# A two-layer recurrent decoder trunk: delayed stores, later residual loads, a third weight buffer and whole-tile output-weight loads

## The chip, the cores and the metric

The kernel runs on one core of one Trainium2 chip. The metric is device time in microseconds of one execution; the runs of the kernel before took 1116.57 us in the median of three (1116.24 to 1118.81). A separate execution was profiled and took 1120.96 us, of which 1119.2 us lie between its first and its last instruction.

## The reference

Two layers are applied to a prompt of 512 tokens and to 8 samples of one token each, with the same weights. Every recurrence is causal and also returns its new state.

```python
def even_layer(h, ...):                       # layer 0
    u = rmsnorm(h, pre_g)
    proj = u @ w_in                           # q,k,v and gates of 8 delta-rule heads, 4 GLA heads
    qkv = silu(causal_conv(...)); q, k = l2norm(q), l2norm(k)
    o1, s_gdn = gated_delta_chunked(q, k, v, beta, log_g, S0)
    o2, s_gla = gla_chunked(q, k, v, log_a, S0)
    o = concat(rmsnorm(o1) * silu(g1), rmsnorm(o2) * silu(g2)) @ w_out
    return h + rmsnorm(o, post_g)

def odd_layer(h, ...):                        # layer 1
    z, xbc, dt = split(rmsnorm(h, pre_g) @ w_in)
    x, B, C = silu(causal_conv(xbc))
    y, s_ssd = ssd_chunked(x, dt, A, B, C, h0)    # 32 heads of 64, 4 groups, state 128
    y = grouped_rmsnorm((y + d * x) * silu(z))
    return h + rmsnorm(y @ w_out, post_g)
```

## The kernel before, in words

**Projections.** All matrix products of the trunk go through `project_half`: a weight tile of 1024 x 128 (eight 128 x 128 blocks) is multiplied with one half of the tokens, 256 or 264 columns, by three products for each block (high part of the weight times high and low part of the activation, low part of the weight times high part: lines 267, 268, 269). That is 24 matmuls for a half and 48 for a tile. A tile comes from memory as one 512 KB load into a `raw` buffer (`load_w`, line 173), of which there are two; `split_w` makes its high part on ScalarE (line 251) and its low part on VectorE or GpSimd (helper `tt`, line 145), into `w` buffers, of which there are five. Output-weight tiles are loaded by `load_wk` (line 228) as two pieces of 256 KB.

**The order of the work.** The program is written per head and per group, but the order in which each engine executes is made when the program is built: a scheduler of the framework sorts every engine's instructions by its own estimate of when they are ready. Each engine then executes its list strictly in that order. All transfers of the kernel are issued by SyncE (SP), so SP's list is one queue: a transfer that has to wait for data or for a free buffer holds up all that stand behind it, weight loads among them. `tc.issue_after(x)` tells the scheduler to place an instruction behind x on x's engine.

**States of the samples.** Each head or pair of heads of the eight samples has a state of 512 KB that is loaded into an `st` buffer, updated and stored from it again. There are two `st` buffers. In layer 0 they hold, in turn, the matrices of `gdn_blocks` (lines 625 to 637, a block inversion that GpSimd does in some 60 small steps), the GLA states (load line 944, use by TensorE line 946, store line 953), and the delta-rule states (load line 770, use line 774, store line 801). In layer 1 `ssd_group` handles four pairs of heads for each of four groups: `sample_state` loads a state (line 1281), multiplies it on GpSimd into `sb` (line 145), scales it on ScalarE (line 1290), adds on VectorE and stores it (line 1292). States of groups 0 to 2 are handled inside the group, those of the last group at the start of the output projection.

**Layer 1, prompt.** In `ssd_group` the inputs of a pair are projected and convolved (`conv`, VectorE line 148), transposed on TensorE (line 1321), scaled by the step (to `ch`, line 1328 or 145), multiplied by the decay on GpSimd (to `ap`), and used in matmuls at lines 1348 and 1361. The normalized outputs of groups 0 to 2 go to a scratch array `ydr` (line 1415), to be read back in the output projection.

**Output projection.** `out_project` contracts 2048 channels in two halves of 1024 (`ks[0]`, `ks[1]`). Layer 0's halves are channels 0 to 3 with 8 to 11 and 4 to 7 with 12 to 15, in units of 128; layer 1's are 0 to 7 and 8 to 15. `mid()` stands between: for layer 0 it handles the last four delta-rule states, then `conv_states` (lines 463 to 470: transposes of the convolution tail through the single PSUM buffer `ps`, a copy to one of two `row` buffers, and stores) and `conv_history` (lines 417 to 420: three small state loads into `st`, each transposed through the same `ps` buffer). `add()` asks for the residual rows that are added at the very end.

Of the kernel before, what the change touches and what calls it, by code (L numbers as in the profile page):

```python
# [16 lines left out]
P = 128  # L17
D = 1024
NK = D // P
TP = 512  # L20
# [37 lines left out]
def kernel(  # L58
# [46 lines left out]
    dma = nc.sync.dma_start  # L105
# [4 lines left out]
    psm = ctx.enter_context(tc.tile_pool(name="psm", bufs=1, space=bass.MemoryType.PSUM))  # L110

    BUFS = {
        "raw": 2, "w": 5, "ua": 16, "ub": 16, "kq": 8, "ap": 8, "vg": 8, "f1": 4, "pre": 3, "inv": 4, "ch": 5, "of": 4, "dec": 5, "hp": 1, "tail": 1, "kqg": 2, "sg": 2,
        "st": 2, "sb": 2, "smc": 6, "smp": 4, "sms": 9, "jk": 1, "c5": 4, "c2": 1, "jd": 1, "nss": 1, "nrs": 1, "ors": 3, "smt": 1, "s1": 3, "u1": 2, "s2": 3, "smh": 6, "sp": 2, "row": 2,
    }
    npo = [0]
    phase = [0]
# [40 lines left out]
    def load_rows(main, extra, tags, between=None):  # L158
# [9 lines left out]
                rows[i].append(xt)  # L168
        return rows

    def load_w(w, row0, col0):
        raw = sb([P, NK, P], tag="raw")
        dma(raw, w[row0:row0 + D, col0:col0 + P].rearrange("(k p) c -> p k c", p=P))
        return raw

    def xblock(rows, i, k):
# [46 lines left out]

    def load_wk(w, ks, col0):
        raw = sb([P, NK, P], tag="raw")
        for h in range(2):
            src = w[ks[4 * h] * P:(ks[4 * h] + 4) * P, col0:col0 + P]
            dma(raw[:, 4 * h:4 * h + 4], src.rearrange("(k p) c -> p k c", p=P))
        return raw

    nsplit = [2]
# [339 lines left out]
    kq, am, eg = {}, {}, {}  # L571
# [468 lines left out]
    def out_project(w, dr, smp, ks, gname, rtags, ptags, mid, add, ltags, share, last, done):  # L1040
# [9 lines left out]
                part.append([t.bitcast(F32) for t in split_tile(ptags[i])])  # L1050
            act.activation(part[i][b], project_half(wts[i], rhs, b), AF.Copy)
        rhs = load_rhs(dr, smp, ks[1], rtags[1], "dec", 2)
        rows = add()
        acc = sb([P, T], tag="ch")
        rs = sb([P, NC + 1], tag="ors")
        low, obs, wts, sqs, ogs, sums = {}, {}, {}, {}, {}, {}
# [9 lines left out]
        for i, b in [(i, b) for i in range(NK - late) for b in range(2)] + [(i, b) for b in range(2) for i in range(NK - late, NK)]:  # L1066
            if b == 0:
                wts[i] = split_w(load_wk(w, ks[1], i * P), *lates.get(i, ()))
            if b == 0 or i >= NK - late:
                sqs[i] = sb([P, T], tag="f1") if i else acc  # L1070
                ogs[i] = sb([P, T], tag="ch")
# [153 lines left out]
    def ssd_group(g):  # L1225
# [52 lines left out]
        def sample_state(j):  # L1278
            pr = 4 * g + j
            st = sb([P, NS, P], tag="st")  # L1280
            dma(st, state_ssd[0, :, 2 * pr:2 * pr + 2].rearrange("b h p n -> (h p) b n"))
            tmp = sb([P, NS, P], tag="sb")
            for q in range(2):
                tt(pool, tmp[:, 4 * q:4 * q + 4], bcb[1][q], st[:, 4 * q:4 * q + 4], MULT)
            dve.reduce_sum(ysr[:, j], tmp, axis=mybir.AxisListType.X)
            tmp = sb([P, NS, P], tag="sb")
            for q in range(2):
                tt(pool, tmp[:, 4 * q:4 * q + 4], bcb[0][q], bc3(xds[:, j, 4 * q:4 * q + 4], P), MULT)
            for b in range(NS):
                act.activation(st[:, b], st[:, b], AF.Copy, scale=sc2[:, 1, pr, b:b + 1])  # L1290
            tt(dve, st, st, tmp, ADD)
            dma(ssd_s[0, :, 2 * pr:2 * pr + 2].rearrange("b h p n -> (h p) b n"), st)
            if j == 3:
                gs = slice(4 * g, 4 * g + 4)
                ya = sb([P, 4, NS], tag="sms")
                tt(pool, ya, ysr, sc2[:, 1, gs], MULT)
                tt(pool, ysm[:, gs], ysm[:, gs], ya, ADD)
                if g % 2 == 1:
                    sample_norm(g)
# [80 lines left out]
        for j in range(4):  # L1380
            pr = 4 * g + j
            y = yt[j][:, 0:TP]
            gt = gts[j]
            el = sb([P, TP], tag="pre")
            for hh in range(2):
                dma(el[hh * 64:hh * 64 + 64, :], ldr[2 * pr + hh:2 * pr + hh + 1, :].to_broadcast([64, TP]))
            act.activation(el, el, AF.Exp)
# [23 lines left out]
        for j in range(4):  # L1411
            y = yt[j][:, 0:TP]
            stt(y, y, vec("ssdg", 4 * g + j, True), rs, MULT, MULT)
            if g < SG - 1:
                dma(ydr[4 * g + j], y)
            else:
                kept[4 * g + j] = yt[j]

# [53 lines left out]
```

## Time and profile before

| | us |
|---|---|
| median of 3 runs | 1116.57 |
| profiled execution | 1120.96 |
| its span, first to last instruction | 1119.2 |
| TensorE matmul busy | 1048.8 |
| TensorE weight load busy | 1006.4 |
| VectorE busy | 720.3 |
| ScalarE busy | 627.4 |
| GpSimd busy | 535.7 |

The mean granted TensorE clock is 0.972. TensorE is busy in 94% of the span, and each of the other engines in 48 to 64%. So a row of another engine matters only where TensorE waited for it. The stages are, in time: layer 0 up to its output projection (to about 490 us), that projection and the norm (to about 700 us), the groups of layer 1 (to about 1046 us), and the last output projection.

A waiting row in the timeline ends in brackets: how long the engine was idle before it, and who released it. In the table of waits the numbers are the total in us, how many times, and the longest.

### The profile page before, as it was taken

Reading aid. Unit: us, or ns where it says so; the run is one execution under the profiler, and the core shown is the slowest. Engines: PE = TensorE matmul, PEld = TensorE weight load, DVE = VectorE, ACT = ScalarE, POOL = GpSimd, SP = SyncE. Lnnn points to the kernel's source line nnn. Section 1 sums busy time; section 2 is a strip of 40 time slices with the busy share of each in tenths; the row PEclk is TensorE's granted clock in tenths of the full one; section 3 lists DMA queues with packets and bytes.
Section 4 is the critical chain, followed back from the end, with each engine's and each line's share of the span. In section 5 each row is a group of like instructions: output and inputs, shape, how many; then the busy total and the mean of one; then the engine's idle time right before and its main releaser. Section 6 shows DMA issues by size and latency. Waiting matters only on the chain.

```text
span 1119.2 us, 23031 instructions
## 1 busy us (share of the span) xinstructions
PE 1048.8 (94%) x8900; PEld 1006.4 (90%) x8900; DVE 720.3 (64%) x1207; ACT 627.4 (56%) x1518; POOL 535.7 (48%) x701
## 2 busy tenths in 40 slices
PE   8999979999989989999889999998999999999997
PEld 7999979899989989889888988898998988989997
DVE  5798353655867754565645366698787688778543
ACT  5566445544444645546233465775686676775452
POOL 4034961304124377114435362386469477468632
PEclk8999999999999989989998999999999999999999
DMA  5234245622554424745563351755657556657632
GB/s 166 81 92 110 72 139 153 194 59 78 171 145 124 110 70 130 217 137 146 160 197 115 100 170 39 210 146 144 188 170 198 181 161 194 206 177 216 187 90 78
DMA packets 241732, 160.01 MB, mean 143 GB/s; under 512 B 21463, under 2 KB 221358, under 8 KB 241606
## 3 DMA queue, kind: packets, MB, share of 16 engines
q1 hardware_dynamic: 241622, 158.53, 48.9%
q8 instruction: 70, 1.15, 0.4%
q14 instruction: 40, 0.33, 0.1%
HBM read 127.05 MB, written 31.84 MB: 142 GB/s over the span
## 4 chain that ended last, share of the span: by engine, by line
PE 40%; DMA 17%; POOL 15%; DVE 13%; ACT 8%; issue 4%; SPq 2%; DVEq 0%; POOLq 0%; ACTq 0%
PE pj L267 9%; PE pj L268 9%; PE pj L269 9%; POOL sb L145 6%; POOL st L145 3%; ACT dec L1343 2%; DVE w L145 2%; DMA sb<-ud 2%; DMA st<-in_state_ssd_dram 2%; DMA out_dram<-st 2%; DVE f L148 1%; DMA pre<-ldr 1%; POOL w L145 1%; DMA inv<-bd 1%; PE px L268 1%
## 5 line engine op out<-in xcount | busy, mean ns | idle before, releaser
L267 PE MATMUL pj<-ua,w 128*128 128x256 f32 x776 | 228.3, 295 | 4.5 <-ACT ua L342 1.7
L269 PE MATMUL pj<-ua,w 128*128 128x256 f32 x776 | 226.9, 293 | 1.2 <-DVE w L145 1.2
L267 PE MATMUL pj<-ub,w 128*128 128x264 f32 x768 | 226.5, 295 | 1.4 <-ACT ub L342 0.9
L269 PE MATMUL pj<-ub,w 128*128 128x264 f32 x768 | 225.7, 294 | 0.0
L268 PE MATMUL pj<-ub,w 128*128 128x264 f32 x742 | 219.0, 295 | 0.0
L268 PE MATMUL pj<-ua,w 128*128 128x256 f32 x750 | 217.7, 291 | 0.0
L145 DVE TENSOR_TENSOR w<-raw,w 128x1024 fp32r<-128x1024 f32 x102 | 136.2, 1335 | 62.9 <-PE pj L268 33.9
L267 PEld LDWEIGHTS pj<-ua,w 128*128 128x128 f32 x776 | 151.3, 195 | 7.4 <-ACT ua L342 2.0
L251 ACT ACTIVATE w<-raw 128x1024 fp32r<-128x1024 f32 x123 | 130.0, 1057 | 46.9 <-DMA raw<-in_o_w_out_dram 11.1
L269 PEld LDWEIGHTS pj<-ua,w 128*128 128x128 f32 x776 | 151.5, 195 | 3.1 <-DVE w L145 1.4
L267 PEld LDWEIGHTS pj<-ub,w 128*128 128x128 f32 x768 | 148.2, 193 | 2.6 <-ACT ub L342 1.1
L269 PEld LDWEIGHTS pj<-ub,w 128*128 128x128 f32 x768 | 148.1, 193 | 1.8 <-issue 1.5
L268 PEld LDWEIGHTS pj<-ua,w 128*128 128x128 f32 x750 | 146.7, 196 | 0.2
L268 PEld LDWEIGHTS pj<-ub,w 128*128 128x128 f32 x742 | 143.3, 193 | 1.6 <-issue 1.1
L145 POOL TENSOR_TENSOR w<-raw,w 128x1024 fp32r<-128x1024 f32 x20 | 49.7, 2484 | 49.1 <-PE px L268 19.4
L145 POOL TENSOR_TENSOR sb<-inv,st 128x512 f32<-128x512 f32 x32 | 54.3, 1714 | 22.7 <-DMA inv<-bd 13.7
L148 DVE SCALAR_TENSOR_TENSOR pf<-xr,cvw,pf 128x512 f32<-128x512 f32 x72 | 54.0, 750 | 11.6 <-ACT pf L440 10.7
L148 DVE SCALAR_TENSOR_TENSOR f<-xr,cvw,f 128x512 f32<-128x512 f32 x72 | 57.6, 799 | 4.3 <-ACT f L440 3.6
L145 POOL TENSOR_TENSOR sms<-sms,sms 128x16 f32<-128x16 f32 (+2 forms) x56 | 22.1, 396 | 77.0 <-ACT sms L960 41.9
L1290 ACT ACTIVATE st<-st,c 128x128 f32<-128x128 f32 x128 | 41.1, 395 | 24.6 <-POOL sb L145 24.6
L439 ACT ACTIVATE xr<-pj 128x256 f32<-128x256 f32 (+1 forms) x72 | 27.3, 380 | 36.7 <-PE pj L269 36.5
L1343 ACT ACTIVATE dec<-dec,c 128x128 f32<-128x128 f32 x128 | 40.5, 390 | 9.8 <-DMA dec<-ldr 8.6
(600 smaller groups left out, 2819.5 us busy)
## 6 DMA issues: line engine op xcount, KB each, us to landing
raw<-in_e_w_in_dram SPq DMA_DIRECT2D x56, 512.0 KB
raw<-in_o_w_in_dram SPq DMA_DIRECT2D x40, 512.0 KB
out_dram<-st SPq DMA_DIRECT2D x32, 512.0 KB
raw<-in_e_w_out_dram SPq DMA_DIRECT2D x32, 256.0 KB
st<-in_state_ssd_dram SPq DMA_DIRECT2D x16, 512.0 KB
dec<-ldr SPq DMA_DIRECT2D x32, 256.0 KB
raw<-in_o_w_out_dram SPq DMA_DIRECT2D x32, 256.0 KB
sb<-vd SPq DMA_DIRECT2D x8, 512.0 KB
```

Source lines behind the costliest of these rows:

```text
L145: eng.tensor_tensor(out, a, b, op=op)
L148: dve.scalar_tensor_tensor(out, a, s, b, op0=op0, op1=op1)
L251: act.activation(wh, rv, AF.Copy)
L267: pe.matmul(ps, wh, uh[b], start=(k == 0), stop=False)
L268: pe.matmul(ps, wh, ul[b], start=False, stop=False)
L269: i0 = pe.matmul(ps, wl, uh[b], start=False, stop=(k == NK - 1))
L439: act.activation(hsl(xr[:, 3:3 + T], b), halves[b], AF.Copy)
L1290: act.activation(st[:, b], st[:, b], AF.Copy, scale=sc2[:, 1, pr, b:b + 1])
L1343: act.activation(rb[:, chunk(c)], rb[:, chunk(c)], AF.Relu, scale=-1.0, bias=lamc[:, c, h:h + 1])
```

## The change

Five edits. (1) The store of a sample state in layer 1 is not issued where it stands; it is placed on SP behind the second weight load that follows (`store_later(2, ...)`), and the store of y to `ydr` behind the next one. The load functions `load_w` and `load_wk` count and release them. (2) `raw` has three buffers in place of two. (3) `st` has three in place of two. (4) A tile of output weights whose eight blocks lie behind each other is one 512 KB load; this holds for both halves of layer 1's projection and for neither half of layer 0's. (5) `add()` is called behind the third weight tile of the second half, not ahead of the first. One broadcast row (`el`, j = 3) takes its buffer from `f1` and not from `pre`.

```diff
-        "raw": 2, ...
-        "st": 2, ...
+        "raw": 3, ...
+        "st": 3, ...
...
+    def run_stores(ld):
+        for s in stores:
+            s[0] -= 1
+        for s in [s for s in stores if s[0] <= 0]:
+            stores.remove(s)
+            with tc.issue_after(ld.ins):
+                s[1]()
...
-        dma(raw, w[row0:row0 + D, col0:col0 + P].rearrange("(k p) c -> p k c", p=P))
+        run_stores(dma(raw, w[row0:row0 + D, col0:col0 + P].rearrange("(k p) c -> p k c", p=P)))
...
-        for h in range(2):
-            src = w[ks[4 * h] * P:(ks[4 * h] + 4) * P, col0:col0 + P]
-            dma(raw[:, 4 * h:4 * h + 4], src.rearrange("(k p) c -> p k c", p=P))
+        for h, n in ((0, NK),) if ks[7] == ks[0] + 7 else ((0, 4), (4, 4)):
+            src = w[ks[h] * P:(ks[h] + n) * P, col0:col0 + P]
+            ld = dma(raw[:, h:h + n], src.rearrange("(k p) c -> p k c", p=P))
+        run_stores(ld)
...
-        rows = add()
...
+                if i == 2:
+                    rows = add()
...
-            dma(ssd_s[0, :, 2 * pr:2 * pr + 2].rearrange("b h p n -> (h p) b n"), st)
+            store_later(2, lambda: dma(ssd_s[0, :, 2 * pr:2 * pr + 2].rearrange("b h p n -> (h p) b n"), st))
...
-            el = sb([P, TP], tag="pre")
+            el = sb([P, TP], tag="pre" if j < 3 else "f1")
...
-                dma(ydr[4 * g + j], y)
+                store_later(1, lambda k=4 * g + j, y=y: dma(ydr[k], y))
```

Since the scheduler sorts the whole program anew, rows move on every engine and from the first microseconds on. Line numbers in rows of the changed kernel are 14 to 16 higher. Three places follow.

In these rows a number behind a name only tells one use of a buffer from another. SP, first GLA heads of layer 0, before. `vd` and `sb` are the samples' values on their way through memory, `odr` a finished head, `st<-in_state_gla` the load of a GLA state, `mdr<-st` the end of `gdn_blocks`, which frees its two `st` buffers.

```order
L931 DMA vd_1855<-row_1853 8x256
L949 DMA sb_1871<-vd_1855 128x1024
L173 DMA raw_2519<-in_e_w_in_dram 128x8x128
L923 DMA odr<-of_1776 128x512
L923 DMA odr<-of_1847 128x512
L944 DMA st_1865<-in_state_gla_dram 128x4x256
L637 DMA mdr<-st_1305 64x1024
L949 DMA sb_1888<-vd_1855 128x1024
L173 DMA raw_2590<-in_e_w_in_dram 128x8x128
```

The same queue now, from the load that starts `gdn_blocks` (`st<-udr`) on:

```order
L640 DMA st_1303<-udr 64x1024
L959 DMA st_1865<-in_state_gla_dram 128x4x256
L187 DMA raw_2252<-in_e_w_in_dram 128x8x128
L187 DMA raw_2320<-in_e_w_in_dram 128x8x128
L187 DMA raw_2379<-in_e_w_in_dram 128x8x128
L922 DMA out_dram<-s_278_1689 128x256
L187 DMA raw_2519<-in_e_w_in_dram 128x8x128
L946 DMA vd_1855<-row_1853 8x256
L964 DMA sb_1871<-vd_1855 128x1024
```

The first GLA state is asked for right behind the load that starts `gdn_blocks`, some five weight loads earlier, into the third buffer.

SP, group 0 of layer 1, before. `out_dram<-st` stores a sample state, `st<-in_state_ssd` loads one, `dec<-ldr` is a broadcast of decays.

```order
L1292 DMA out_dram<-st_9358 128x8x128
L173 DMA raw_9779<-in_o_w_in_dram 128x8x128
L173 DMA raw_9846<-in_o_w_in_dram 128x8x128
L1281 DMA st_9619<-in_state_ssd_dram 128x8x128
L1292 DMA out_dram<-st_9557 128x8x128
L173 DMA raw_9960<-in_o_w_in_dram 128x8x128
L1281 DMA st_9638<-in_state_ssd_dram 128x8x128
```

Now, at the first store of the same group:

```order
L1357 DMA dec_9592<-ldr 128x512
L1308 DMA out_dram<-st_9358 128x8x128
L1297 DMA st_9636<-in_state_ssd_dram 128x8x128
L187 DMA raw_9843<-in_o_w_in_dram 128x8x128
L187 DMA raw_9960<-in_o_w_in_dram 128x8x128
L1357 DMA dec_9600<-ldr 128x512
L1308 DMA out_dram<-st_9557 128x8x128
L187 DMA raw_10027<-in_o_w_in_dram 128x8x128
L1297 DMA st_10437<-in_state_ssd_dram 128x8x128
```

Three states are loaded ahead of this place where it were two, so the load behind the first store is that of the group's fourth state and not of its third; it stands directly behind the store whose buffer it takes, with two weight loads behind it.

TensorE, layer 0's output projection, before: transposes of the convolution history (`ps<-ident,st`) among other work.

```order
L420 MATMUL ps_7156<-ident,st_7154 128x24 x8
L713 MATMUL pr_6832<-u_1215_6822,ch_6717 128x128
L720 MATMUL pf_6726<-u_1215_6822,ap_4536 128x128
L268 MATMUL pj_7816<-ap_7689,w_7776 128x264
L269 MATMUL pj_7816<-kq_7688,w_7777 128x264
L420 MATMUL ps_7173<-ident,st_7171 128x24 x8
```

Now, with the transposes of the convolution tail (`ps<-ident,tail`), which stood tens of rows apart:

```order
L478 MATMUL ps_7132<-ident,tail_572 72x128
L478 MATMUL ps_7137<-ident,tail_572 96x128
L1098 MATMUL po_7761<-ident,ch_7760 128x128
L1098 MATMUL pf_7762<-ident,ch_7760 128x128
L478 MATMUL ps_7145<-ident,tail_572 96x128
L435 MATMUL ps_7156<-ident,st_7154 128x24 x8
L435 MATMUL ps_7173<-ident,st_7171 128x24 x8
L282 MATMUL pj_7796<-kq_7686,w_7756 128x264
```

Five users of the one `ps` buffer stand behind each other, with two small transposes as the only other work.

More of the change, by code (lines that the diff above doesn't have):

```diff
@@ L112 @@
     BUFS = {
-        "raw": 2, "w": 5, "ua": 16, "ub": 16, "kq": 8, "ap": 8, "vg": 8, "f1": 4, "pre": 3, "inv": 4, "ch": 5, "of": 4, "dec": 5, "hp": 1, "tail": 1, "kqg": 2, "sg": 2,
-        "st": 2, "sb": 2, "smc": 6, "smp": 4, "sms": 9, "jk": 1, "c5": 4, "c2": 1, "jd": 1, "nss": 1, "nrs": 1, "ors": 3, "smt": 1, "s1": 3, "u1": 2, "s2": 3, "smh": 6, "sp": 2, "row": 2,
+        "raw": 3, "w": 5, "ua": 16, "ub": 16, "kq": 8, "ap": 8, "vg": 8, "f1": 4, "pre": 3, "inv": 4, "ch": 5, "of": 4, "dec": 5, "hp": 1, "tail": 1, "kqg": 2, "sg": 2,
+        "st": 3, "sb": 2, "smc": 6, "smp": 4, "sms": 9, "jk": 1, "c5": 4, "c2": 1, "jd": 1, "nss": 1, "nrs": 1, "ors": 3, "smt": 1, "s1": 3, "u1": 2, "s2": 3, "smh": 6, "sp": 2, "row": 2,
     }
@@ L169, in load_rows, with store_later @@
         return rows
+    stores = []
+    def store_later(n, f):
+        stores.append([n, f])
+    def run_stores(ld):
[5 more added lines that the diff above has]
+                s[1]()
     def load_w(w, row0, col0):
         raw = sb([P, NK, P], tag="raw")
-        dma(raw, w[row0:row0 + D, col0:col0 + P].rearrange("(k p) c -> p k c", p=P))
+        run_stores(dma(raw, w[row0:row0 + D, col0:col0 + P].rearrange("(k p) c -> p k c", p=P)))
         return raw
```

## The prediction

> **What bounds the kernel now.** The first view is the profile page: the span, the busy time of each engine, and the shares of the chain of work that ended last.
>
> ```profile
> span 1119.2 us, 23031 instructions
> PE 1048.8 (94%) x8900; PEld 1006.4 (90%) x8900; DVE 720.3 (64%) x1207; ACT 627.4 (56%) x1518; POOL 535.7 (48%) x701
> PE 40%; DMA 17%; POOL 15%; DVE 13%; ACT 8%; issue 4%; SPq 2%; DVEq 0%; POOLq 0%; ACTq 0%
> ```
>
> TensorE is busy for 1048.8 of 1119.2 us, so 70.4 us are all that better cover can win in idle time. The chain is misleading by itself: it gives 17% to DMA and 15% to GpSimd, but most of that is work that TensorE does not wait for, since there is always a projection beside it. The second view is therefore the table of waits of TensorE alone: what it waited for, the total in us, how many times, the longest.
>
> ```profile
> PE pr L1321 <- DVE kq L148: 6.5, 4, 2.1
> PE ps L946 <- DMA st<-in_state_gla_dram: 4.8, 3, 3.6
> PE ps L774 <- DMA st<-in_state_gdn_dram: 4.6, 2, 3.1
> PE px L656 <- DVE inv L647: 3.9, 1, 3.9
> PE pr L1361 <- POOL ap L145: 3.8, 2, 3.3
> PE pj L269 <- DVE w L145: 2.2, 2, 1.2
> ```
>
> No single wait is large. Weights, the most frequent thing that TensorE needs, cost it 2.2 us in all; two kinds of state load cost 4.8 and 4.6. The change can win at the waits that end in a state load or in what a state load sets going, and it can lose wherever the new order puts users of one buffer close together. I take each of those places in the timeline and look at the granted clock behind it, since a wait here is followed by some microseconds at half clock.
>
> **The change part by part.** The profiled execution took 1120.96 us: its span of 1119.2 and 1.76 around it. That is 4.39 above the median of 1116.57, so I make the sum against 1120.96 and take 4.39 off at the end.
>
> First, the third `st` buffer at the first GLA state. The first row is from the chain of waits, the second from TensorE's timeline, the third from the windows (length, busy time of PE, PEld, DVE, ACT and POOL, granted clock, DMA share, GB/s).
>
> ```profile
> 159.89 4.04 DMA st<-in_state_gla_dram
> 163.98 1.08 PE L946 MATMUL ps<-st,sms 128*32 128x256 f32 x8 [3.61 <-DMA st<-in_state_gla_dram]
> 163.00:170.00 7.00, 6.02 (x31) 5.21 (x32) 2.25 (x5) 2.76 (x5) 0.37 (x2) 0.51 1.06 318
> ```
>
> The load began at 159.89, because both buffers belonged to `gdn_blocks` until its last store, and TensorE idled 3.61 us for it. Behind it TensorE was busy 6.02 us at a clock of 0.51, which cost 6.02 x 0.49 = 2.9. In the changed order the load stands right behind `st<-udr`, before the inversion starts, so 4.04 us of loading lie under that inversion. Term: -3.61 - 2.9 = -6.5. What is late next is the rest of that head, whose values come by SP; nothing of it shows as a wait here.
>
> Second, the delta-rule state at 315 us.
>
> ```profile
> 305.23 5.60 DMA out_dram<-st
> 310.85 4.18 DMA st<-in_state_gdn_dram
> 315.17 0.41 PE L774 MATMUL ps<-st,c 128*32 128x128 f32 x4 [3.14 <-DMA st<-in_state_gdn_dram]
> 317.00:320.50 3.50, 3.50 (x23) 2.89 (x22) 0.41 (x2) 0.38 (x1) 1.90 (x1) 0.54 0.37 150
> ```
>
> The store of 5.60 us and the load of 4.18 stand in series on one buffer. With three buffers the load does not wait for that store, and it can start up to 5.60 us earlier, more than the 3.14 us of idling. The 3.50 us at 0.54 behind it cost 3.50 x 0.46 = 1.6. Term: -4.7. Here stands a rule to weigh. The Trainium skill ("TensorE: Matmul & The Clock Gate", section "HAM oscillation — how this bites in real kernels") has TensorE throttled after idle gaps longer than about 3.4 us. By that rule this gap of 3.14 us and the one of 3.29 below would have kept full clock, 1.6 and 1.7 us would not be there to win, and the sum would be -11.2, a median of 1105.4; the trace shows 0.54 and 0.52 behind them, so I go by the trace.
>
> Third, two smaller waits for state loads of the same kinds.
>
> ```profile
> 445.37 0.64 PE L946 MATMUL ps<-st,sms 128*32 128x256 f32 x8 [0.75 <-DMA st<-in_state_gla_dram]
> 562.83 0.65 PE L774 MATMUL ps<-st,c 128*32 128x128 f32 x16 [1.42 <-DMA st<-in_state_gdn_dram]
> ```
>
> Any load that starts 1.42 us earlier removes both. Term: -2.2.
>
> Fourth, group 0 of layer 1: five rows of the chain, the wait that they end in, and its window.
>
> ```profile
> 734.40 3.59 DMA out_dram<-st
> 738.00 6.83 DMA st<-in_state_ssd_dram
> 744.97 1.87 POOL sb L145
> 757.53 3.97 POOL sb L145 x2
> 762.66 1.01 POOL ap L145
> 763.72 0.64 PE L1361 MATMUL pr<-ap,kqg 128*128 128x128 f32 x2 [3.29 <-POOL ap L145]
> 764.00:767.50 3.50, 3.50 (x18) 3.50 (x18) 2.84 (x4) 1.99 (x10) 3.42 (x6) 0.52 1.02 281
> ```
>
> The third sample state of the group waits for the store of the first (3.59), is loaded (6.83), and is then multiplied on GpSimd, whose list is in strict order: the prompt's `ap` stands behind those multiplications and TensorE waits 3.29 us for it. Now the third state is loaded before the group begins, at least 3.59 us earlier. Term: 3.29 + 3.50 x 0.48 (1.7) = -5.0. What is late next is VectorE's convolution; three more small waits of the same groups hang on similar chains.
>
> ```profile
> 750.92 0.66 PE L1321 MATMUL pr<-ident,kq 128*128 128x128 f32 x4 [1.70 <-DVE kq L148]
> 829.11 1.09 PE L1348 MATMUL po<-dec,ch 128*64 128x128 f32 x16 [1.17 <-DVE ch L145]
> 845.45 0.73 PE L1348 MATMUL po<-dec,ch 128*64 128x128 f32 x5 [1.19 <-ACT ch L1328]
> ```
>
> Together 4.1 us, which I leave where they are and use only for the low end.
>
> Fifth, the one place where the new order looks worse: the single `ps` buffer in layer 0's output projection.
>
> ```profile
> 597.13 2.58 DMA out_dram<-row
> 600.17 0.67 PE L420 MATMUL ps<-ident,st 24*128 24x24 f32 x8
> 602.38 0.64 PE L420 MATMUL ps<-ident,st 24*128 24x24 f32 x8 [0.65 <-DVE sms L145]
> 606.60 1.01 PE L420 MATMUL ps<-ident,st 24*128 24x24 f32 x8 [1.42 <-DMA st<-in_state_ssd_conv_dram]
> 603.00:614.00 11.00, 9.12 (x47) 8.39 (x47) 5.71 (x17) 2.70 (x8) 4.09 (x7) 0.53 0.22 64
> ```
>
> From one history transpose to the next the hand-over of `ps` took 600.17 to 602.38, 2.2 us, most of it covered by other work; the bare waits are 0.65 and 1.42, 2.1 in all. Now five users stand behind each other with two small transposes between. With no cover I count one history hand-over of 2.2, one wait for a `row` buffer to be stored (2.58), and two tail copies at the bare 0.65 (the nearest row for one): 6.1 against 2.1, so +4.0. The half clock behind it (9.12 x 0.47 = 4.3) is there either way. Bounds: if the cluster is covered after all, the waits and the half clock go, -2.1 - 4.3 = -6.4; if each of the four hand-overs costs the whole 2.58, 10.3 - 2.1 = +8.2. I take +4.0.
>
> Then the edits at nothing. Third `raw` buffer and delayed stores, by SP's waits:
>
> ```profile
> SPq L173 <- DVE w L145: 217.3, 57, 10.3
> SPq L1292 <- DVE st L145: 51.9, 15, 8.7
> SPq L1281 <- DMA out_dram<-st: 24.1, 11, 3.9
> ```
>
> SP waits 217.3 us in 57 loads for the split that frees a raw buffer, 3.8 us each: weight loads are early, not late, and TensorE's 2.2 us of waiting for `w` are all that earlier loads can win (bound -2.2, taken 0). A store of a sample state that moves behind two weight loads no longer blocks SP for the addition (51.9 us in 15 waits), but it holds its `st` buffer for longer; the third buffer pays for that. One 512 KB load in place of two of 256 KB takes eight issues off SP for each half of layer 1's projection, a queue that waits anyway. For the residual rows I use the pace of a projection:
>
> ```profile
> 734.76 0.29 PE L267 MATMUL px<-ua,w 128*128 128x256 f32 x1
> ...
> 736.44 0.28 PE L269 MATMUL px<-ua,w 128*128 128x256 f32 x1
> ```
>
> Fourteen steps in 1.68 us are 0.12 each, 5.8 for the 48 of a tile. Asked for behind the third of eight tiles and added at the end, the rows have nearly 29 us of TensorE's work as cover; if that were gone, a load like the 4.18 above would show once. `el` in `f1` moves a load of no consequence to TensorE.
>
> Left uncounted is one more wait, for the inversion of a block.
>
> ```profile
> 477.80 0.64 PE L656 MATMUL px<-inv,ap 32*32 32x32 f32 x16 [3.87 <-DVE inv L647]
> ```
>
> Its inputs pass through memory by SP, and the new order may shorten or keep it: -3.9 to 0, taken 0.
>
> Sum: -6.5 - 4.7 - 2.2 - 5.0 + 4.0 = -14.4; 1120.96 - 14.4 = 1106.6 profiled, and 1102.2 as a median.
>
> **The rivals.** A larger gain: the `ps` cluster is covered (its +4.0 and the 2.1 that stay, together 6.1, do not come), the three waits of 4.1 and the 3.87 of the inversion go: 1102.2 - 6.1 - 4.1 - 3.9 = 1088.1. For it: all of them are ends of chains through SP or GpSimd, which the change relieves. Against: the kernel has ready work elsewhere at none of them.
>
> No change: each state load was only the last of several things that were late, and the next is just behind. At 763.72 this is GpSimd's own list (3.97 us for two multiplications), which the change does not shorten; at 163.98 the samples' values by SP. If two thirds of the 18.4 us won come back, 12.3 of them, the median is 1102.2 + 12.3 = 1114.5; I allow 1113 to 1118. For it: only 40% of the chain is TensorE's, the rest is spread over DMA and three engines. Against: the two large waits name loads of 4 us that stood alone at the end.
>
> Slower: SP is blocked by state loads. In the changed order of groups 0 to 2, twelve loads into `st` (three of them read back `ydr`) stand behind the store of the very buffer that they take, with at most one weight load between; SP then waits at the load until the store has landed, 3.59 to 5.60 us, mean 4.6, with weight loads queued behind. Before, such blocks at layer 1's loads took 24.1 us in 11 waits, 2.2 each. The extra is 2.4 each, 29 us, if no lead is left; with a lead of 3.8 (above) only 4.6 - 3.8 = 0.8 each, 10 us, reach TensorE. With the middle, 19.5, and layer 0's terms (-6.5 - 4.7 - 2.2 + 4.0 = -9.4) as forecast, the time is 1116.6 - 9.4 + 19.5 = 1126.7; the bounds give 1117 to 1136, and it decides against the change once blocks cost more than 9.4 + 3.3 = 12.7 us. For it: stores are later by design, hence closer to the load that needs the buffer. Against: the third `raw` buffer adds lead just there, and the 24.1 us before cost TensorE almost nothing. The Trainium skill ("DMA: Bandwidth & Descriptors", section "Anatomy of one DMA — SWDGE (gpsimd) path") says that any wait for a semaphore happens on the sequencer that issues, and not in the DMA engines; the row of 24.1 us on SP agrees.
>
> **How the numbers follow.** About 0.3%, 3.3 us, is what a measurement of this kernel can tell from no change, so faster means below 1113.2 and slower above 1119.9. The forecast has 0.50; its own range is 1092 (6.1 and 4.1 more won) to 1109.4 (the second and third term, 6.9, not won, a little more at `ps`). The larger gain has 0.12, no change 0.18, slower 0.20. Faster is then 0.62. The range runs from 1087, just below the larger gain's centre, to 1122, which leaves out about half of the larger gain (0.06) and most of the slower case (0.14).
>
> **What would show it.** In the waits of the changed kernel, TensorE's rows for L946 and L774 (now 14 to 16 lines lower) released by state loads should be gone or under 1 us, the wait at the first `ap` matmul of group 0 too, and the granted clock in the microseconds behind those places near full. A wait cluster of about 6 us at the transposes of tail and history should appear in layer 0's output projection. SP's waits for the addition before a state's store should shrink, and its waits for `out_dram<-st` at layer 1's state loads should grow without a `w` or `raw` wait of TensorE beside them. I am wrong if the state waits stay or hand on to DVE or POOL at the same length, if TensorE's waits on `w` rise from 2.2 to over 12 us, or if the time is won at places not named here.

## The result, and the profile after

The changed kernel took 1129.53 us (median of 6 runs, 1125.51 to 1134.91) beside 1116.99 us for the kernel before (6 runs): ratio 1.0106, 95% interval 1.0082 to 1.0130. Run again beside other kernels it took 1126.17 us, ratio 1.0082 (1.0054 to 1.0110). It is slower by about 1%, where 1102.2 us had been forecast, and lies above the stated range. Its profiled execution took 1128.63 us.

The page of the changed kernel, span and busy times:

```profile
span 1126.8 us, 22981 instructions
...
PE 1052.8 (93%) x8900; PEld 1004.9 (89%) x8900; DVE 716.3 (64%) x1207; ACT 626.1 (56%) x1518; POOL 538.1 (48%) x701
```

TensorE does the same 8900 matmuls, and its idle time in the span went from 70.4 to 74.0 us. The table of TensorE's waits shows that this is not the old idle time:

```profile
PE px L671 <- DVE inv L662: 6.7, 3, 3.8
PE po L1098 <- ACT ch L1095: 6.3, 2, 5.6
PE pr L1377 <- POOL ap L145: 3.0, 2, 2.0
PE pj L284 <- DVE w L145: 1.5, 2, 1.0
PE ps L961 <- DMA st<-in_state_gla_dram: 1.1, 2, 0.7
```

The waits for GLA states fell from 4.8 to 1.1 us, and those for delta-rule states (4.6 before) have no row left. In their place stand the inversion with 6.7 (3.9 before) and, new, 6.3 us at the transposes of the output projection's sum (line 1098).

The places of the forecast's first and fourth term, in TensorE's timeline and the windows (granted clock after the counts of POOL):

```profile
161.16 0.64 PE L961 MATMUL ps<-st,sms 128*32 128x256 f32 x8 [0.72 <-DMA st<-in_state_gla_dram]
163.00:170.00 7.00, 6.48 (x59) 6.09 (x58) 4.31 (x8) 4.86 (x14) 1.11 (x6) 1.00 0.52 154
768.65 0.53 PE L1364 MATMUL po<-dec,ch 128*64 128x128 f32 x3 [1.23 <-ACT ch L1344]
771.00:778.00 7.00, 7.00 (x61) 7.00 (x61) 5.31 (x9) 3.94 (x7) 4.59 (x4) 1.00 0.27 77
849.68 0.71 PE L1377 MATMUL pr<-ap,kqg 128*128 128x128 f32 x4 [1.95 <-POOL ap L145]
```

The first GLA state is waited for 0.72 us and not 3.61, with full clock behind it (0.51 before). In group 0 of layer 1 the wait of 3.29 us for `ap` is gone and the clock is 1.00; TensorE waits 1.23 us there for another thing, ScalarE's `ch`. In group 1 it now waits 1.95 us for the same kind of `ap`.

And the place that was named as the only bad one, layer 0's output projection, in the timelines of TensorE, VectorE, ScalarE and SP, and its window:

```profile
594.88 0.27 PE L478 MATMUL ps<-ident,tail 128*72 128x128 f32 x1
595.58 0.32 PE L478 MATMUL ps<-ident,tail 128*96 128x128 f32 x1 [0.42 <-ACT row L480]
601.46 0.47 PE L1098 MATMUL po<-ident,ch 128*128 128x128 f32 x1 [5.57 <-ACT ch L1095]
601.73 0.42 PE L1098 MATMUL pf<-ident,ch 128*128 128x128 f32 x1
601.94 0.42 PE L478 MATMUL ps<-ident,tail 128*96 128x128 f32 x1
602.73 1.04 PE L435 MATMUL ps<-ident,st 24*128 24x24 f32 x8 [0.36 <-ACT row L480]
```
```profile
599.00 1.23 DVE L145 TENSOR_TENSOR sb<-sb,sms 128x1024 f32<-128x1024 f32 x1 [6.41 <-DMA sb<-ud]
600.14 0.41 DVE L145 TENSOR_TENSOR kq<-kq,pj 128x256 f32<-128x256 f32 x1
```
```profile
600.59 0.42 ACT L1094 ACTIVATE ch<-kq 128x256 f32<-128x256 f32 x1 [5.07 <-DVE kq L145]
600.92 0.49 ACT L1095 ACTIVATE ch<-kq,vcol 128x256 f32<-128x256 f32 x1
```
```profile
590.66 0.29 SPq L810 DMA_DIRECT2D ud<-row  x1
594.62 0.36 SPq L812 DMA_DIRECT2D sb<-ud  x1
```
```profile
601.00:612.00 11.00, 9.09 (x57) 8.28 (x58) 4.72 (x16) 2.20 (x8) 2.15 (x5) 0.60 0.25 69
```

Read from the bottom: the last delta-rule state of the samples sends a row through memory. SP issues its store at 590.66 and the load that reads it back at 594.62; VectorE can multiply at 599.00, after 6.41 us of idling. Right behind that product in VectorE's list stands the first addition of the projection's two halves (`kq<-kq,pj`), whose last input, a projection half of TensorE, was there at about 595.0. ScalarE scales it, and TensorE, with nothing else in front in its list, waits 5.57 us for it, between two users of the `ps` buffer. The clock behind it is 0.60 over 11 us (0.53 over 11 us before).

One execution has its own few microseconds, so stages are compared over several. The measure is when TensorE's n-th matmul starts (the records of each kernel in the table hold 8900; since the lists are in different orders, it is a fair measure only where the same matmuls lie ahead in all of them). At the 5200th this is so. At the 4800th, 20 to 28 matmuls still differ: small ones of the heads stand ahead of it where before has matmuls of projections. From the mean steps in these traces, 0.13 us for a projection matmul and about 0.1 for a small one, I estimate that this is worth 0.4 to 0.6 us. Means over the profiled executions of kernels that share an order in layer 0, the experiments below included:

| | 4800th | 4800th to 5200th | 5200th to last | last |
|---|---|---|---|---|
| two `st`, two `raw` (before, e3, e4) | 584.8 | 54.4 | 473.1 | 1112.3 |
| three `st`, two `raw` (e1, e7) | 576.5 | 58.6 | 478.7 | 1113.7 |
| two `st`, three `raw` (e2, e8, e15, e16) | 579.5 | 55.3 | 473.8 | 1108.5 |
| three of both (changed, e5, e6, e13) | 577.6 | 62.8 | 477.0 | 1117.4 |

The 4800th matmul lies just ahead of the projection's second half. The changed kernel is 7.2 us ahead there, gives back 8.4 in the next 400 matmuls (61.6 to 64.2 in its four executions, 53.6 to 55.5 in the three of before), and loses 3.9 from there to the end. At the 5200th matmul, where the lists have met, each third buffer alone is 4.1 or 4.4 us ahead of before, and the two together are 1.2 behind. These profiles differ by 5.1 us and the medians of the changed kernel by 9 to 12.5, so they hold about half of the loss. Most of the rest is the choice of the execution: the profiled ones of before, e3 and e4 lie 2.4 to 4.3 us above the medians of their kernels, the four of the last row between 1.0 below and 1.8 above.

### The profile page after: what moved, and what is told of

It reads as the page before. It is cut to its first block, busy times and chain, and to the rows that moved or that the text cites. A ratio compares the mean times of both kernels' runs of the same rounds, so it can differ in the third digit from the quotient of the medians.

```text
span 1126.8 us, 22981 instructions
## 1 busy us (share of the span) xinstructions
PE 1052.8 (93%) x8900; PEld 1004.9 (89%) x8900; DVE 716.3 (64%) x1207; ACT 626.1 (56%) x1518; POOL 538.1 (48%) x701
## 5 line engine op out<-in xcount | busy, mean ns | idle before, releaser
L282 PE MATMUL pj<-ua,w 128*128 128x256 f32 x776 | 225.2, 291 | 3.8 <-ACT ua L1046 1.6
L284 PE MATMUL pj<-ua,w 128*128 128x256 f32 x776 | 223.7, 289 | 0.0
L283 PE MATMUL pj<-ua,w 128*128 128x256 f32 x750 | 217.0, 290 | 0.5 <-POOL ua L1047 0.3
L145 DVE TENSOR_TENSOR w<-raw,w 128x1024 fp32r<-128x1024 f32 x102 | 139.7, 1370 | 52.5 <-PE pj L283 33.4
L282 PEld LDWEIGHTS pj<-ua,w 128*128 128x128 f32 x776 | 148.5, 192 | 6.0 <-ACT ua L1046 2.0
L284 PEld LDWEIGHTS pj<-ua,w 128*128 128x128 f32 x776 | 149.4, 193 | 1.8 <-issue 1.3
L283 PEld LDWEIGHTS pj<-ua,w 128*128 128x128 f32 x750 | 144.3, 192 | 2.0 <-issue 0.5
L266 ACT ACTIVATE w<-raw 128x1024 fp32r<-128x1024 f32 x123 | 129.7, 1055 | 21.0 <-PE pj L284 11.2
L145 POOL TENSOR_TENSOR sb<-inv,st 128x512 f32<-128x512 f32 x32 | 56.0, 1765 | 10.4 <-DMA inv<-bd 9.2
L145 POOL TENSOR_TENSOR sms<-sms,sms 128x16 f32<-128x16 f32 (+2 forms) x56 | 17.2, 308 | 59.2 <-DVE sms L145 38.7
```

Source lines behind the costliest of these rows:

```text
L145: eng.tensor_tensor(out, a, b, op=op)
L266: act.activation(wh, rv, AF.Copy)
L282: pe.matmul(ps, wh, uh[b], start=(k == 0), stop=False)
L283: pe.matmul(ps, wh, ul[b], start=False, stop=False)
L284: i0 = pe.matmul(ps, wl, uh[b], start=False, stop=(k == NK - 1))
```

## The experiments

After the result my theory was that the third `st` buffer wins what was forecast and another part of the change takes it away. First each part alone, beside the same runs of before (1118.25 us, 32 runs). The third state buffer:

```diff
-        "st": 2, ...
+        "st": 3, ...
```

> The kernel before with only the third st buffer. My theory now: the third st buffer does what was forecast for layer 0 (the waits for state loads go, 7 to 11 us by the end of layer 0's heads), and the loss comes from the other edits' order, so this kernel alone is faster than before: 1106 to 1113 us. On VectorE the first addition of the two halves in layer 0's output projection stands 16 rows behind the last sample product, so the wait of 5.57 us at the transposes of that sum does not come. Rival: the third st buffer itself does the harm by the new order, 1122 to 1130 us.

Measured: 1120.98 us, ratio 1.0024 (1.0003 to 1.0045): not the gain of my theory, and not the size of the rival; a difference of 0.2% is also what two equal programs show (e3 below). The table shows why it is not faster: 8.3 us ahead at the 4800th matmul, 4.2 given back in the projection, 5.6 lost from there to the end.

The third raw weight buffer:

```diff
-        "raw": 2, ...
+        "raw": 3, ...
```

> The kernel before with only the third raw buffer. My theory: it brings TensorE's and VectorE's work on the second half of layer 0's output projection forward, to two rows behind the last sample product that waits for a round trip through memory; TensorE then waits about 5 us there and runs 10 us at half clock, and no state wait goes: 1121 to 1130 us, slower than before. Rival: earlier weight loads win or cost nothing, 1114 to 1119 us, and the loss is elsewhere.

Measured: 1112.36 us, ratio 0.9949 (0.9925 to 0.9972). My theory was wrong: this part alone makes the kernel faster. The wait of 5 us at the sum is 1.24 here, though the addition stands only two rows behind the product.

The delayed stores alone (`store_later` and `run_stores`, all buffers and loads as before):

> The kernel before with only the delayed stores of sample states and of y; all buffers as before. Layer 0 is in the same order as before. Rival of the forecast (SP blocked by state loads right behind the stores of their buffers): slower by 8 us or more, 1125 us and above, since with two st buffers each load must wait for a later store. My theory: the stores cost little, within 4 us of before, 1114 to 1121 us.

Measured: 1116.82 us, ratio 0.9979 (0.9955 to 1.0002). On all five engines this kernel's order is that of before, row for row, apart from the numbers in names: the stores stood behind those loads already. With two `st` buffers the first edit does nothing, and the difference of 0.2% is what two equal programs show.

The one-piece output weight loads, the later residual rows and `el` in `f1`:

> The kernel before with only the one-piece output weight loads, the residual rows asked for later and one broadcast row in another buffer. Both theories: within 3 us of before, 1114 to 1120 us. If it is over 1122 us, the residual rows or the whole loads are the cause, which no theory here has.

Measured: 1118.51 us, ratio 1.0004 (0.9979 to 1.0029). Nothing, as expected.

Multiplied, the four ratios give 0.9956. The changed kernel is at 1.008 to 1.011, so some parts cost together what none costs alone. The next four leave parts out, beside 1117.32 us for before (23 runs). The changed kernel unchanged:

> The changed kernel once more, beside the three kernels that leave one part of it out. 1125 to 1132 us, about 1.0% above before; its stage times against the first profile show which of the stage differences are the program's and which are those of one execution.

Measured: 1126.17 us, 1.0082 (1.0054 to 1.0110); the wait at the sum is 5.04 us in its profile.

Both third buffers in the kernel before (`"st": 3`, `"raw": 3`), nothing else:

> The kernel before with both third buffers and nothing else. Its order in layer 0 is that of the changed kernel row for row. Theory: it is the two buffers together that bring TensorE's, VectorE's and SP's work of layer 0's output projection into the bad order, so this kernel is as slow as the changed one: 1124 to 1132 us. Rival: the loss is in layer 1 and comes from the buffers together with the later residual rows, one-piece loads or the moved broadcast; then it is 1112 to 1119 us.

Measured: 1124.13 us, 1.0075 (1.0049 to 1.0101). The two buffers make the loss. Its profile has the same wait:

```profile
PE po L1082 <- ACT ch L1079: 6.0, 3, 5.0
```

The changed kernel with `"raw": 2`:

> The changed kernel with two raw buffers. Theory (the two buffers together): the first addition on VectorE stands 16 rows behind the last sample product as with the st buffer alone, and the time is near that one's, 1117 to 1123 us. Rival (layer 1's edits with the third st buffer): 1125 to 1132 us.

Measured: 1119.83 us, 1.0011 (0.9993 to 1.0030). And with `"st": 2`:

> The changed kernel with two st buffers. Theory: near the third raw buffer alone, 1110 to 1117 us, faster than before. Rival (layer 1's edits with the third raw buffer do the harm): 1122 us and above.

Measured: 1114.91 us, 0.9984 (0.9963 to 1.0005). Either buffer taken out brings the time back to before; these two, e5 and e6 agree that it is the pair.

The next four, beside 1117.08 us (27 runs), ask what happens in the projection. First the product and sum of the last sample state on GpSimd:

```diff
-            tt(dve, ubc, ubc, bc3(kn[:, j], C), MULT)
-            tt(dve, st, st, ubc, ADD)
+            e = pool if h == 7 else dve
+            tt(e, ubc, ubc, bc3(kn[:, j], C), MULT)
+            tt(e, st, st, ubc, ADD)
```

> The changed kernel with the last sample state's product and sum on GpSimd and not on VectorE; the order of all else in layer 0's output projection stays as in the changed kernel (TensorE's is the same row for row there). Theory (VectorE's list waits for the last sample's round trip through memory, and the first sum of the two halves stands right behind it): the wait of 5.0 to 5.6 us at the transposes of that sum goes or falls under 1.5 us, and with the half clock behind it 6 to 9 us are won: 1117 to 1123 us. Rival (the users of the one ps buffer set the time there, as forecast): the wait moves to the tail or history transposes and the time stays at 1124 to 1130 us.

Measured: 1124.92 us, 1.0076 (1.0049 to 1.0102). The wait at the sum is gone (0.51), and the time is the same. The rival's wait stands in its place, in TensorE's and ScalarE's timelines of this kernel:

```profile
600.92 1.05 PE L435 MATMUL ps<-ident,st 24*128 24x24 f32 x8 [3.98 <-ACT row L480]
603.66 1.01 PE L435 MATMUL ps<-ident,st 24*128 24x24 f32 x8 [1.69 <-issue]
605.68 1.02 PE L435 MATMUL ps<-ident,st 24*128 24x24 f32 x8 [1.01 <-DVE sms L145]
```
```profile
600.60 0.27 ACT L480 ACTIVATE row<-ps 96x128 f32<-96x128 f32 x1 [4.09 <-DMA out_dram<-row]
```

The third copy of the tail out of `ps` waits 4.09 us for a `row` buffer to be stored. This is the cluster of the forecast, hidden behind the sum until now.

The last state's update read from an older scratch (`uds[4]` in place of its own `ud`), so that nothing waits for the store; the kernel leaves out this state's own update by that:

```diff
-            dma(ubc, ud.unsqueeze(0).to_broadcast([P, NS, C]))
+            uds.append(ud)
+            dma(ubc, uds[4 if h == 7 else h].unsqueeze(0).to_broadcast([P, NS, C]))
```

> The changed kernel with the last sample state's update read from the scratch of the first of the last four states, written long before, so its load waits for no store (this state's new value is left wrong by that). Theory: the product on VectorE is ready several us earlier, the wait at the transposes shrinks by the round trip, 4 us, and 4 to 8 us are won: 1118 to 1124 us. Rival (the ps buffer): no change, 1124 to 1130 us.

Measured: 1124.48 us, 1.0057 (1.0037 to 1.0078). No wait above 1.34 us is left in the cluster, and the 400 matmuls take 60.0 us and not 62.8. That is the direction of the theory, but against the run beside it (1.0076) the gain is within the intervals: inconclusive. The order moved too: the first addition stands 14 rows behind the last sample product here, and directly behind it in the changed kernel.

Two tries for a faster version: three raw buffers, and a third state buffer of its own tag in layer 0 only, for every other delta-rule state, or for the GLA states:

```diff
-            st = sb([P, NS, C], tag="st")
+            st = sb([P, NS, C], tag="st" if h & 1 else "sx")
...
-            st = sb([P, 4, 256], tag="st")
+            st = sb([P, 4, 256], tag="sx")
```

> The kernel before with three raw buffers and a third state buffer that only every other delta-rule state of layer 0 uses; layer 1 keeps two. On VectorE the first sum of the halves stands 32 rows behind the last sample product, as before the change. Theory (the third raw buffer wins, a third state buffer wins in layer 0 as long as the projection's order stays, and costs in layer 1): 1105 to 1113 us, the fastest so far. Rival (any third state buffer costs what it wins): 1117 to 1122 us.

> The same with the third buffer for the GLA states of layer 0 alone, so that the first of them is loaded ahead of the block inversion; on VectorE the first sum stands 13 rows behind the last sample product. Theory: the first term (6.5 us) is won, the wait of 5 us at the transposes does not come or is under 3 us, layer 1 keeps two buffers: 1107 to 1115 us. Rival: the projection's wait comes back, 1118 us and above.

Measured: 1118.68 us, 1.0003 (0.9982 to 1.0024), and 1119.00 us, 1.0018 (0.9996 to 1.0039). Neither beats the third raw buffer alone; both rivals were nearer. The second has the wait for the row store back, 5.19 us at the history transposes.

Then a third `row` buffer (`"row": 2` to `"row": 3`), which leaves the order of every engine as it is, in the changed kernel and in the one with the product on GpSimd, and beside them the third raw buffer with and without it (before: 1117.24 us, 23 runs):

> The changed kernel with a third row buffer; every engine's order is that of the changed kernel, row for row. Theory (two chains end at the same place in layer 0's output projection, the first sum behind the last sample product on VectorE and the users of the ps buffer behind the row stores, and either alone sets the time): no change, the wait of 5 us at the transposes of the sum stays, 1124 to 1130 us. Rival (the row stores set it, the sum was only named last): 3 us or more won, 1118 to 1122 us.

> The changed kernel with the last sample product and sum on GpSimd and a third row buffer; the order is that of the kernel with the product on GpSimd, row for row. Theory: both chains are cut, the waits of 4.0 and 1.7 us at the history transposes and of 5 us at the sum go, with the half clock behind them 5 to 9 us are won: 1116 to 1121 us. Rival (the loss is not in this place): 1124 to 1130 us with both waits gone.

Measured: 1124.30 us, 1.0072 (1.0050 to 1.0093), with the wait at the sum still 4.88 us, as expected. And 1125.55 us, 1.0082 (1.0052 to 1.0112), with both waits gone and a third one in their place, at the last of the history transposes:

```profile
604.58 1.01 PE L435 MATMUL ps<-ident,st 24*128 24x24 f32 x8 [3.72 <-DVE sms L145]
```

The profile names VectorE's reading of `ps`, which went on until 604.5 behind two sums of 1.9 and 2.2 us (0.2 us in the changed kernel), each beside one of the two operations that had been moved to GpSimd (rows at the end). My theory of two chains did not hold: there are at least three. The rival's time came true, but with a third wait in the same place this does not yet say that the loss is elsewhere.

> The kernel before with three raw and three row buffers; the order is that of the third raw buffer alone, row for row. There the second kind of wait stood with 2.7 us at the history transposes. Theory: 2 to 4 us less than the third raw buffer alone, 1107 to 1112 us, the fastest version. Rival: no change against it.

> The kernel before with only the third raw buffer once more, as the measure for the run beside it with three row buffers: 1110 to 1115 us, 0.3 to 0.7% faster than before.

Measured: 1113.94 us, 0.9969 (0.9947 to 0.9991), and 1113.44 us, 0.9969 (0.9948 to 0.9990). The third row buffer adds nothing to the third raw buffer, which alone is confirmed as faster than before; the wait of 1.92 us for the row store in e16's profile is gone in e15's, and that at the sum stands at 3.25 us and not 1.64. It is the best version found.

Last, the history left out of two kernels: the changed one with the product on GpSimd and three row buffers (e14), and the kernel before:

```diff
-        hpo.append(conv_history(state_ssd_conv, cvw[1], "hpo"))
+        hp = sb([P, 24, NS], tag="hp")
+        pool.memset(hp, 0.0)
+        hpo.append(hp)
```

> The changed kernel with the last sample product on GpSimd and three row buffers, and the convolution history of layer 1 left out (its buffer is set to zero, so the samples' layer 1 is wrong by that): all three chains at layer 0's output projection are cut there. Its partner is the kernel before with the same part left out. Theory (the loss is that place): the stretch is as long as the partner's within 2 us, and the two kernels' times differ by less than 4 us, where the changed kernel and before differ by 7 to 12. Rival (the loss is elsewhere, in layer 1): the difference stays 7 us or more.

> The kernel before with the convolution history of layer 1 left out (set to zero). It loses the half clock and the short waits at the history transposes: 1110 to 1117 us by both theories; what counts is its difference to the run beside it.

Measured beside 1117.10 us (23 runs): 1121.80 us, 1.0042 (1.0020 to 1.0064), and 1118.96 us, 1.0019 (0.9998 to 1.0041). The difference is 2.8 us, where e14, the first of the two with its history, and before differ by 8.3; that part of the theory held. The partner missed its range of 1110 to 1117 us: it is 1.9 us above before, so that part of the smaller difference comes from there. The other part of the theory did not hold: the stretch is not as long as the partner's, since a fourth wait stands in it, now for the samples' columns of the projection's input, in TensorE's timeline:

```profile
597.16 0.80 PE L282 MATMUL pj<-kq,w 128*128 128x264 f32 x2 [6.85 <-ACT kq L1047]
```

So four different waits took each other's place there. What they have in common is in the order. The last transposes of the prompt's heads on TensorE, and the moment when ScalarE splits the samples' columns (which end the chain of sample states), in before:

```profile
604.07 1.11 PE L733 MATMUL pr<-ident,ch 128*128 128x128 f32 x4 [0.46 <-DVE ch L145]
```
```profile
597.06 0.74 ACT L1031 ACTIVATE kq<-dec 128x264 fp32r<-128x264 f32 x2 [1.49 <-POOL dec L1027]
```

and the same two in the changed kernel:

```profile
586.82 0.66 PE L748 MATMUL pr<-ident,ch 128*128 128x128 f32 x4 [0.50 <-DVE ch L145]
```
```profile
605.39 0.74 ACT L1046 ACTIVATE kq<-dec 128x264 fp32r<-128x264 f32 x2 [2.72 <-POOL dec L1042]
```

Before, the sample chain ended 7 us ahead of the prompt's heads, which covered it. Now the heads end 17 us earlier and the chain 8 us later, so 18.6 us lie between the two, with only projection tiles as cover, and TensorE runs into whichever link of the chain its list names next. In the four executions with both buffers the chain ends 17 to 19 us behind the heads; in those of one third buffer 13 to 14 behind, and they lose 0.9 us (`raw`) and 4.2 us (`st`) in this stretch. The distance alone does not give the loss: in e12 it is 12.6 us, and the stretch is as long as the changed kernel's, 63.1 us.

## Why the prediction was wrong, point by point

By the table's means the sum of -14.4 us came out as +5.1. Of the 19.5 us between, 6.2 lie ahead of the 4800th matmul (-13.4 forecast, -7.2 measured), 4.4 in the projection (+4.0 and +8.4) and 8.9 behind it (-5.0 and +3.9). Three steps failed. At the waits for states, each wait that goes was counted as time won, with what is late next at nothing: about half of layer 0's terms arrived, and nothing of layer 1's. In the projection the term was half of what came, because the wait at the sum was missing from it. And the forecast had no term for what the third state buffer costs at the end of layer 1, about 4 us.

**Each state load, first three terms.** Right in mechanism: the waits at the first GLA state and at the delta-rule states went, with the clock behind them. Of the 13.4 us forecast 7.2 arrived by the 4800th matmul (8.3 with the third `st` buffer alone). At the 3186th matmul, at about 390 us, where the same matmuls lie ahead in these kernels and the first two terms (11.2 us) should be won, the third `st` buffer alone is 7.8 us ahead and the changed kernel 3.9. New waits stand in the changed kernel's profile, 2.94 us at 91 us and 2.11 at the inversion at 470 among them. The forecast looked at each place for what is late next and not at other places.

**The users of `ps`, +4.0.** The place was right, and the size was 8.4 by the table, or about 8 with the 0.5 us for the order at the 4800th taken off, twice the term and at its upper bound of 8.2. No rival had this place as worse. What I had read was the row order of TensorE alone; I took the work beside the cluster, the transposes of the first sum, as ready. It was not: VectorE's list has the addition directly behind the last sample product (in before 34 rows behind), and that product waits for a store and a load. Behind it stands the order: the prompt's heads, which were the cover of the samples' chain, end at 583 to 591 us in every kernel of the table with a third buffer of either kind, and at 599 to 604 in the three of before. The samples' chain ends at 591 to 597 us in before's three, 597 to 603 with one third buffer and 603 to 608 with both. This is not only the time won at state loads: with the third `raw` buffer alone the states are waited for 5.4 and 3.5 us in all (e2), and the heads end as early. That the lost cover is the common root is argued from these end times and from e10 and e17; no run shortened the whole chain.

**Group 0 of layer 1, -5.0.** The wait for `ap` went, and the clock there is 1.00, but nothing was won. In nine executions with three `st` buffers in layer 1 the way from the 5200th matmul to the last is 477.5 us in the mean, in nine with two 473.2, so the third buffer costs about 4 us there. The same traces say where. The two means differ by 0.5 us up to the 7350th matmul (at about 912 us), by 0.9 up to the 7900th (984), by 3.4 up to the 8350th (1044) and by 4.3 up to the last. So groups 0 to 2, which end at 961 us in before, are level within 1 us, the wait of 1.95 us in group 1 included, and the loss lies in the last group and the output projection. What sets it there is not shown.

**Edits at nothing.** Right for the stores, the loads in one piece, the residual rows and `el`. Wrong for the third raw buffer, whose gain was bounded by TensorE's 2.2 us of waits on `w`: alone it wins 0.3 to 0.5%, 3.8 and 5.9 us in its two measurements, and the profiles of its order are 5.3 us ahead at the 4800th matmul and 3.8 at the last. A buffer count is not only a time at which a load may start; here it reorders the whole program. Which of the two wins the time is not shown.

**The slower rival.** It named SP blocked at state loads of layer 1. SP's waits in the changed kernel:

```profile
SPq L1308 <- DVE st L145: 43.6, 15, 6.1
SPq L812 <- DMA ud<-row: 19.6, 8, 3.7
SPq L1297 <- DMA out_dram<-st: 19.5, 8, 4.1
```

At the loads of states they fell from 24.1 to 19.5 us. At the loads that read `ydr` back into `st`, which the rival counted too, they rose from 2.1 to 10.4 us. SP's waits behind 700 us, in before and in the changed kernel:

```profile
SPq L1025 <- DMA out_dram<-st: 2.1, 2, 1.4
```
```profile
SPq L1040 <- DMA out_dram<-st: 10.4, 3, 3.8
```

Both kinds of load together are 3.7 us more, where the rival had 10 to 29. TensorE's waits on VectorE's `w` fell from 2.2 to 1.5 us, those on GpSimd's rose from 0.2 to 2.6 (one of 2.38 is shown below). So the sign came true, and at most a small part of it by this mechanism. The chance of 0.20 was too small: nothing in the working priced the risk that a program sorted anew loses cover somewhere else.

**A slip in a sum.** -14.4 + 1.6 + 1.7 is -11.1 and not -11.2; the forecast does not use it.

**What stays open.** What makes the third state buffer cost some 3 to 4 us behind 984 us, and whether a shorter chain of the samples would give the projection's 8 us back.

## What to carry to other kernels

Where a scheduler sorts the whole program, a change of buffers is a change of order: ask not only which wait goes, but which serial chain used to lie under the work that is now done earlier, and compare the two end times. Try the parts of a change alone and in pairs before a chain is blamed; here one part won 0.3 to 0.5%, one was level within the 0.2% that equal programs differ by, and the two together lost 0.7 to 1.1%. And a wait that goes without a clear gain, as in e9, e10 and e14 in one place, says that the named releaser is only the last of several.

## What the runs showed of the hardware that was not expected

A row of 8 x 128 values took from 590.66 to 599.00 us to go through memory and back to VectorE, 8.3 us, half of it until SP went on behind the landed store. Beside it, in the work that ends in the samples' columns, GpSimd raises a 128 x 32 tile to a power in 5.42 us; this last one of its kind takes 5.4 us in all the profiles:

```profile
593.04 5.42 POOL L145 TENSOR_TENSOR sms<-sms,nhalf 128x32 f32<-128x32 f32 x1
```

Work moved to GpSimd can hold VectorE. In e14's timelines of VectorE and GpSimd:

```profile
599.77 1.94 DVE L145 TENSOR_TENSOR hp<-hp,sms 128x64 f32<-128x64 f32 x1
602.01 2.21 DVE L145 TENSOR_TENSOR hp<-hp,sms 128x64 f32<-128x64 f32 x1
604.51 0.23 DVE L145 TENSOR_TENSOR hp<-hp,sms 128x64 f32<-128x64 f32 x1
```
```profile
599.73 1.89 POOL L145 TENSOR_TENSOR sb<-sb,sms 128x1024 f32<-128x1024 f32 x1 [0.16 <-DMA sb<-ud]
601.80 2.34 POOL L145 TENSOR_TENSOR st<-st,sb 128x1024 f32<-128x1024 f32 x1
```

A sum of 0.23 us takes 1.94 and 2.21 when it starts beside a GpSimd operation, and ends with it. The Trainium skill ("SBUF — State Buffer", section "SBUF: two separate sides") says that VectorE with two inputs in SBUF and a GpSimd operation exclude each other for a whole instruction, and the rows agree. So e14 traded a wait for a memory round trip for this one; in e9 one such sum took 0.90 us, at 602.40, and ended with GpSimd's second operation.

The clock fell behind a gap of 2.38 us. In the changed kernel's timeline and window:

```profile
735.01 0.39 PE L284 MATMUL px<-ua,w 128*128 128x256 f32 x1 [2.38 <-POOL w L145]
736.00:739.50 3.50, 3.50 (x19) 3.50 (x19) 3.50 (x4) 3.50 (x9) 3.50 (x4) 0.51 1.05 287
```

The forecast weighed the Trainium skill's bound of about 3.4 us ("TensorE: Matmul & The Clock Gate", section "HAM oscillation — how this bites in real kernels") against gaps of 3.14 and 3.29 and went by the trace; this gap of 2.38 us with a clock of 0.51 behind it speaks the same way. The length of one gap does not decide it here: behind one of 2.98 us, which ends at 406.37 in the same profile, the clock is 1.00 from 406.0 to 409.5.

Two programs with the same order on every engine (before and e3) came out at a ratio of 0.9979 with 12 runs against 32; a difference of 0.2% says nothing here.
